# Three head pairs' queries and keys kept in SBUF, a reordered first chunk of products, and one scaling moved from ScalarE to VectorE, in a hybrid attention and pooling block

## The chip, the cores and the metric

The kernel runs on one core of a Trainium2 chip. A core has five engines that run their own instruction streams side by side: TensorE (PE, matrix products; the load of its weights is listed apart as PEld), VectorE (DVE), ScalarE (ACT), GpSimd (POOL) and SyncE (SP, which here only issues transfers). Transfers run on 16 DMA engines. SBUF is the on-chip memory of 128 partitions, PSUM holds the results of the products, DRAM is outside. The metric is the time of one execution in device microseconds, lower is better.

## The reference

One block over 1024 tokens of width 1024, all in float32. The input is normed and projected; the projection's columns feed latent attention of 8 heads (64 plain and 32 rotary dimensions, causal by chunks of 64 tokens), a pooling branch over trailing windows, and gates. Both branches are gated, projected, merged, projected once more, added to the input and normed.

```python
def mla_attention(zq, zkv, zkr, q_norm, w_uq, kv_norm, w_ukv):
    c_q = rms_norm(zq, q_norm)
    q = jnp.einsum('bsr,rhd->bshd', c_q, w_uq)
    q_nope = q[..., :QK_NOPE_DIM]                      # 64 dims
    q_rope = apply_rope(q[..., QK_NOPE_DIM:], ...)     # 32 dims
    kv = jnp.einsum('bsr,rhd->bshd', rms_norm(zkv, kv_norm), w_ukv)
    k_nope, v = kv[..., :QK_NOPE_DIM], kv[..., QK_NOPE_DIM:]
    k_rope = apply_rope(zkr, ...)
    # per block of 128 queries: softmax(mask((qn.kn + qr.kr) * scale)) @ v

def reference(...):
    z = jnp.einsum('bsd,de->bse', rms_norm(x, norm_in), w_in)
    zq, zkv, zkr, g_attn, u_pool, g_pool, g_merge = jnp.split(z, IN_SPLITS, axis=-1)
    y_attn = mla_attention(...) * silu(g_attn)
    y_pool = multiscale_pool(u_pool, ...) * silu(g_pool)
    merged = gate_a * (y_attn @ w_branch_attn) + gate_p * (y_pool @ w_branch_pool)
    return rms_norm(x + merged @ w_out, norm_final)
```

## The kernel before, in words

Every float32 product is made of three products of rounded halves: an operand is split into a rounded part (names `wh`, `hi`, `uh`, `kh`, `qh`, made on ACT at L298) and the rest (`wl`, `lo`, `ul`, `kl`, `ql`, made on DVE at L308), and h·h, h·l and l·h are summed in PSUM (`mms`, L275).

The program's stages in order of time: the first products, `zq`, over eight chunks of the input (0 to some 45 us); the input projection and the pooling branch (to some 360 us); the queries and keys of the four head pairs and the values (`run_up`, `run_rope`, `run_v`, to 394 us); attention head by head (from 394 us to some 555 us), into whose gaps the pooling branch's products `pf` (weights `w_bp`, one piece for each head) are laid; the attention branch's projection, the output projection and the final norm.

The order on each engine comes from `Plan.order` (L127 to L202). It simulates the program with a cost for each operation and takes, on each engine, among the operations that could start within 30 ns of the first the one that stands first in the program. SBUF tiles come from tags with a fixed number of slots (L25): `t`, 45 tiles of 128x1024, `wr` and others. Slots of a tag are handed out in the order in which the program first names the tiles; so a late tile holds up those behind it. `wr` has one slot: the next weight piece can be loaded only when VectorE has made the `wl` of the piece before it. `wh` and `wl` have two each.

All loads and stores of `dma` (L372 to L383, the rows say L378) are issued by SP in this one order, so an issue that waits holds up all behind it. An SP issue also waits until the transfer eight places before it has landed.

The **first chunk**, n = 0 (L610 to L630): x comes in two halves of 512 tokens. ACT makes the rounded half (`xa` left, `xb` right), DVE the rest into the same tiles, and PE multiplies with the rounded weights `wqh` and the rest `wql`. There are 18 products of 128x512: three parts (wh·h, wh·l, wl·h), two halves, three column groups (`ps`, `ps`, `pb`).

**Queries and keys** (`run_up`, L822 to L850): for each pair p of heads the product lies in PSUM, is split into `uh` and `ul` of 128x1024 (64 partitions for each head), and these are written to DRAM (`qn_d`, `kn_d`). Head 0's half goes to the heads' operand tiles straight from `uh` and `ul`. There are two sets of operand tiles (`heads[0]`, `heads[1]`: `qh`, `ql`, `kh`, `kl`); `load_head` (L811) fills the set of head h, 64 partitions from `qn_d` and `kn_d` and 32 from the rotary part. The loads of a head stand in the order behind the last score product of the head that used the set before.

**Attention's start**: each head has score products `sc`, their maxima on DVE (L357), exponentials `pr` on ACT (L290), a scaling on POOL (L322), transposes `pt` on PE (L282), the transposed tile's split `pT` (ACT L298, DVE L308), and the products `o` with the values.

**The end** (`finish`, L1288): two row blocks `res` are left; the one before the last is scaled by one over its norm and written out, while the last still gets its final piece (`pb`, added on DVE) and its squares (`junk`, on ACT).

Of the kernel before, what the change touches and what calls it, by code (L numbers as in the profile page):

```python
# [10 lines left out]
AF = mybir.ActivationFunctionType  # L11
ALU = mybir.AluOpType
AX = mybir.AxisListType

P = 128
# [4 lines left out]
QK_DIM = 96  # L20
Q_RANK = 384
KV_RANK = 256
N_BG = 4
WARM = 8
SLOTS = {"t": 45, "wr": 1, "wh": 2, "wl": 2, "go": 2, "oa": 2, "s": 2, "p": 2, "o": 1, "f": 1}  # L25
PSUM = "spof"
# [183 lines left out]
def hybrid_block_kernel(  # L210
# [42 lines left out]
    def dram(rows, name, cols=T):  # L253
        b = Buf(lambda: tc.dram_tile([rows, cols], F32, name=name), None)
        return View(b, 0, rows, 0, cols)
# [217 lines left out]
    mask_d = dram(64, "mask_d")  # L473
    kr_d = [dram(32, f"kr_d{i}") for i in range(2)]
    qr_d = [[dram(P, f"qr_d{t}{i}") for i in range(2)] for t in range(2)]
    qn_d = [[dram(P, f"qn_d{p}{i}") for i in range(2)] for p in range(4)]
    kn_d = [[dram(P, f"kn_d{p}{i}") for i in range(2)] for p in range(4)]
    gate_d = [dram(P, f"gate_d{t}") for t in range(16)]
    y_d = [dram(P, f"y_d{t}") for t in range(4)]
    gp_d = [dram(P, f"gp_d{t}") for t in range(4)]  # L480
# [78 lines left out]
    zq_acc = [Acc("s"), Acc("s"), Acc("pp")]  # L559
# [44 lines left out]
    for n, k in enumerate(ORDER):  # L604
        w, x = raws[k]
        wh, wl = buf("wh", 1024, F32R, "wqh"), buf("wl", 1024, F32R, "wql")
        xa, xb = tr("xa"), tr("xb")
        if k < 4:
            xs[k] = ((xa[:, :512], xb[:, :512]), (xa[:, 512:], xb[:, 512:]))
            step_n = 512  # L610
        else:
            xs[k] = ((xa[:, :512], xa[:, 512:]), (xb[:, :512], xb[:, 512:]))
            step_n = T
        for a in range(0, T, step_n):
            c = slice(a, a + step_n)
            h, l = (xs[k][0][a // 512], xs[k][1][a // 512]) if k < 4 else (xa, xb)
            act(h, x[:, c], AF.Copy, scale=gin[k])
            if a == 0:
                if n == 0:
                    vcopy(wh[:, :Q_RANK], w[:, :Q_RANK])  # L620
                    tt(wl[:, :Q_RANK], w[:, :Q_RANK], wh[:, :Q_RANK].f32(), ALU.subtract)
                else:
                    split(wh[:, :Q_RANK], wl[:, :Q_RANK], w[:, :Q_RANK])
            stt(l, x[:, c], gin[k], h.f32(), ALU.mult, ALU.subtract)
        if n + 3 < 8:
            raws[ORDER[n + 3]] = start_loads(ORDER[n + 3])
        h, l = xs[k]
        for a, b, f, e in ((wh, h, n == 0, False), (wh, l, False, False), (wl, h, False, n == 7)):
            for hf in range(2):
                mms([(zq_acc[c].halves[hf], a[:, 128 * c : 128 * c + 128], b[hf], f, e) for c in range(3)])  # L630
    for n in range(4):
        B.setdefault("b11", []).append((xs[n][0][0], xs[n][1][0]))
        B.setdefault("b21", []).append((xs[4 + n][0][0], xs[4 + n][1][0]))
# [177 lines left out]
    def load_head(h):  # L811
        d = heads[h % 2]
        p, r = h // 2, 64 * (h % 2)
        load_rope(h)
        for x, n in enumerate("hl"):
            dma(d["q" + n][0:64, :].f32(), qn_d[p][x][r : r + 64, :])
            dma(d["k" + n][0:64, :].f32(), kn_d[p][x][r : r + 64, :])

    def run_up(p, which, first):
        def run(it):  # L820
            acc = next_acc()
            cs = state["cq"] if which == "q" else state["ckv"]  # L822
            n = len(cs)
            if first:
                shared[which] = (it.h, it.l)
            if which == "q" and p == 0:
                for g in range(4):
                    yp[g] = t32("y")
                    dma(yp[g], y_d[g])
                load_mp(0)  # L830
            if which == "k" and p == 1:
                dress_slots(heads[0])
                load_rope(0)
                load_mp(1)
            wh, wl = shared[which]
            o = n * (p if which == "k" else p % 2)
            prod(acc, wh[o : o + n], wl[o : o + n], halves(cs))
            h, l = tr("uh"), tr("ul")
            for ps, a, b in acc.spans:
                split(h[:, a:b], l[:, a:b], ps)  # L840
            dst = qn_d if which == "q" else kn_d
            if p == 0:
                if which == "q":
                    make_slots()
                dma(heads[0][which + "h"][0:64, :].f32(), h[0:64, :].f32())
                dma(heads[0][which + "l"][0:64, :].f32(), l[0:64, :].f32())
            r = 64 if p == 0 else 0
            dma(dst[p][0][r:P, :], h[r:P, :].f32())
            dma(dst[p][1][r:P, :], l[r:P, :].f32())
        return run  # L850

    def run_rope(t):
# [274 lines left out]
    q, kv = Latents("q"), Latents("kv")  # L1127
# [129 lines left out]
    class Rows:  # L1257
# [31 lines left out]
        def finish(self, e, last=False):  # L1289
            r, ss, st = self.t[e], self.ss[e], self.st[e]  # L1290
# [7 lines left out]
            if last and not e:  # L1298
                act(r[:, rgt], r[:, rgt], AF.Copy, scale=st)
                stt(r[:, 256:512], r[:, 256:512], st, nf[:, 256:512], ALU.mult, ALU.mult)  # L1300
                ts(r[:, :256], r[:, :256], st, None, ALU.mult)
            elif last:
                act(r, r, AF.Copy, scale=st)
            else:
                stt(r, r, st, nf, ALU.mult, ALU.mult)
            for c in (lft, rgt):
# [145 lines left out]
    for h in range(HEADS):  # L1452
# [7 lines left out]
        for qr in range(4):  # L1460
            prs = []
            for i in (2 * qr, 2 * qr + 1):
                nk = 128 * (i + 1)
                ps = buf("s", T, F32, "sc")
                q = slice(128 * i, 128 * i + 128)
# [135 lines left out]
```

## Time and profile before

| what | value |
|---|---|
| runs (us) | 701.85, 703.6, 706.39; median 703.6 |
| the profiled execution's own time | 702.37 us |
| its span | 700.2 us, 9698 instructions, mean granted clock 0.991 |
| PE busy | 682.6 us (97%) |
| DVE, ACT, POOL busy | 539.6 (77%), 355.9 (51%), 116.8 us (17%) |
| written to DRAM / read from DRAM | 46.27 MB / 93.73 MB |

Times inside the trace count from the span's start. A row of a timeline gives the start, how long one instruction took (x8: eight together), engine, line, operation, the tile written and the tiles read, and in brackets the idle time of the engine before it and the work that it waited for. The rows that the prediction uses stand in the section behind the change.

### The profile page before, as it was taken

To read this page: it belongs to the slowest core of one execution; us is meant where nothing else is said; L and a number is where in the kernel's file an instruction comes from. 1 tells how busy PE (TensorE), PEld (TensorE's weight loads), DVE (VectorE), ACT (ScalarE), POOL (GpSimd) and SP (SyncE) were. 2 spreads that over 40 slices of the span, in tenths; PEclk is the share of its full clock that TensorE was granted. 3 is DMA by queue.
4 is the path that set the end of the run, shared out by engine and by line. 5 is a ranking of instruction groups with operands and counts; after the bars stand their busy time and mean duration, and the time that the engine had idled before them with its cause. 6 is when DMAs were issued, how large, how long until landed. Compare 5 with 4: busy or idle time off the path is not lost.

```text
span 700.2 us, 9698 instructions
## 1 busy us (share of the span) xinstructions
PE 682.6 (97%) x3368; PEld 574.3 (82%) x3368; DVE 539.6 (77%) x868; ACT 355.9 (51%) x660; POOL 116.8 (17%) x153
## 2 busy tenths in 40 slices
PE   8999999999999999999999979999999999999995
PEld 6878888888888888888888769999899888878784
DVE  5687997668878578669958757877887889967883
ACT  5864524442444354443545546677676673334433
POOL 0020100300003030300001034444444300000000
PEclk9999999999999999999999989999999999999998
DMA  8947656361977539364778982554540389984612
GB/s 314 383 163 278 208 208 189 82 189 59 316 238 191 176 126 321 85 191 149 293 240 301 331 190 62 147 145 112 122 121 31 106 288 372 303 270 134 203 68 90
DMA packets 55871, 136.42 MB, mean 195 GB/s; under 512 B 5904, under 2 KB 17296, under 8 KB 55696
## 3 DMA queue, kind: packets, MB, share of 16 engines
q1 hardware_dynamic: 53568, 131.63, 56.0%
q0 software_dynamic: 2256, 4.20, 4.2%
q8 instruction: 26, 0.43, 0.3%
q14 instruction: 21, 0.17, 0.1%
HBM read 93.73 MB, written 46.27 MB: 200 GB/s over the span
## 4 chain that ended last, share of the span: by engine, by line
PE 88%; DMA 4%; DVE 3%; issue 2%; ACT 1%; SPq 1%; DVEq 0%; ACTq 0%
PE pb L275 36%; PE ps L275 31%; PE sc L275 6%; PE pf L275 5%; PE o L275 5%; PE pt L282 4%; PE pv L275 2%; DMA kh<-kr_d 1%; DMA wr<-w_bp 1%; SPq L378 1%; DMA x<-xT 1%; DVE mr L308 1%; DMA mr<-m_d 1%; DVE small L357 0%; DVE res L308 0%
## 5 line engine op out<-in xcount | busy, mean ns | idle before, releaser
L275 PE MATMUL pb<-t,wp 128*128 128x512 f32 x504 | 121.3, 389 | 0.0
L275 PEld LDWEIGHTS pb<-t,wp 128*128 128x128 f32 x504 | 94.4, 188 | 19.5
L298 ACT CAST wp<-wr 128x512 fp32r<-128x512 f32 x98 | 59.4, 620 | 94.6 <-PE ps L275 53.3
L308 DVE TENSOR_TENSOR wp<-wr,wp 128x512 fp32r<-128x512 f32 x98 | 71.9, 747 | 36.8 <-ACT wp L298 35.5
L275 PE MATMUL ps<-xa,wp 128*128 128x512 f32 x224 | 73.8, 389 | 0.0
L322 POOL TENSOR_SCALAR pr<-pr,small 128x128 f32<-128x128 f32 (+3 forms) x64 | 48.7, 765 | 77.3 <-DVE small L348 68.9
L290 ACT ACTIVATE pr<-sc,small 128x128 f32<-128x128 f32 (+3 forms) x64 | 47.6, 745 | 19.3 <-DVE small L357 16.4
L308 DVE TENSOR_TENSOR pT<-pt,pT 128x512 fp32r<-128x512 f32 (+1 forms) x80 | 48.8, 633 | 8.9 <-ACT pT L298 8.3
L357 DVE TENSOR_REDUCE small<-sc 128x1 f32<-128x128 f32 (+3 forms) x64 | 47.3, 750 | 9.8 <-PE sc L275 9.2
L298 ACT CAST pT<-pt 128x512 fp32r<-128x512 f32 (+1 forms) x80 | 41.5, 544 | 25.5 <-PE pt L282 24.5
L275 PE MATMUL o<-pT,v 128*128 128x256 f32 (+1 forms) x320 | 48.4, 286 | 2.0 <-ACT pT L298 1.5
L275 PEld LDWEIGHTS ps<-xa,wp 128*128 128x128 f32 x224 | 42.0, 188 | 8.7
L275 PEld LDWEIGHTS o<-pT,v 128*128 128x128 f32 x320 | 44.8, 193 | 4.8 <-ACT pT L298 1.9
L275 PE MATMUL ps<-xb,wp 128*128 128x512 f32 x112 | 43.6, 389 | 0.0
L282 PE MATMUL pt<-ident,pr 128*128 128x128 f32 x288 | 42.6, 276 | 0.3 <-DVE pT L308 0.3
L275 PE MATMUL pb<-wo,wp 128*128 128x512 f32 (+1 forms) x180 | 40.5, 376 | 0.2 <-DVE res L308 0.2
L275 PE MATMUL pb<-xa,wp 128*128 128x512 f32 x168 | 40.7, 389 | 0.0
L275 PE MATMUL ps<-t,wp 128*128 128x512 f32 x168 | 40.7, 390 | 0.0
L275 PE MATMUL sc<-kh,qh 128*128 128x384 f32 (+4 forms) x96 | 36.2, 377 | 2.9 <-ACT pr L290 2.8
L275 PEld LDWEIGHTS pb<-wo,wp 128*128 128x128 f32 x180 | 32.4, 188 | 7.0 <-issue 0.5
L275 PEld LDWEIGHTS pb<-xa,wp 128*128 128x128 f32 x168 | 31.5, 188 | 6.5
L275 PEld LDWEIGHTS ps<-t,wp 128*128 128x128 f32 x168 | 31.5, 188 | 6.5
(207 smaller groups left out, 1446.5 us busy)
## 6 DMA issues: line engine op xcount, KB each, us to landing
wr<-w_z SPq DMA_DIRECT2D x30, 512.0 KB, 5.3
gate_d<-z SPq DMA_DIRECT2D x16, 512.0 KB, 3.5
xt<-xr SPq DMA_DIRECT2D x8, 512.0 KB, 9.8
mp<-gate_d SPq DMA_DIRECT2D x8, 512.0 KB, 6.5
gate<-gate_d SPq DMA_DIRECT2D x8, 512.0 KB, 7.4
wo<-wt_d SPq DMA_DIRECT2D x8, 512.0 KB, 9.2
m_d<-gate SPq DMA_DIRECT2D x16, 256.0 KB, 5.7
mr<-m_d SPq DMA_DIRECT2D x16, 256.0 KB, 4.5
```

Of the source, the lines that this page charges most:

```text
L275: nc.tensor.matmul(real(o), real(a), real(b), start=s, stop=e, **kw)
L282: nc.tensor.transpose(real(o), real(a), real(ident))
L290: nc.scalar.activation(real(o), real(x), func, scale=real(scale), **kw)
L298: lambda: nc.scalar.copy(real(o), real(x)),
L308: plan.add(eng, lambda: e.tensor_tensor(real(o), real(a), real(b), op), c, [a, b], [o], port=port)
L322: e.tensor_scalar(real(o), real(a), real(s1), real(s2), op0, op1)
L357: lambda: nc.vector.tensor_reduce(real(o), real(a), axis=AX.X, op=ALU.max, negate=True),
L378: lambda: nc.sync.dma_start(real(o), real(x)),
```

## The change

Three edits. The first chunk's 18 products are written in the program with all three parts of the left half of the tokens first, then all three of the right half (the planner still chooses the order on the engine, below). The queries and keys of head pairs 0 to 2 are no longer written to DRAM: their `uh` and `ul` (12 tiles of the tag `t`) stay in SBUF, and `load_head` copies 64 partitions of them into the heads' operand tiles; pair 3 is written to DRAM and read back as before. The row block before the last is scaled on VectorE (`ts`) where ScalarE (`act`) did it.

```diff
@@ -20,7 +20,7 @@
 QK_DIM = 96
 Q_RANK = 384
 KV_RANK = 256
-N_BG = 4
+KEPT = 3
 WARM = 8
 SLOTS = {"t": 45, "wr": 1, "wh": 2, "wl": 2, "go": 2, "oa": 2, "s": 2, "p": 2, "o": 1, "f": 1}
 PSUM = "spof"
@@ -473,8 +473,8 @@
     mask_d = dram(64, "mask_d")
     kr_d = [dram(32, f"kr_d{i}") for i in range(2)]
     qr_d = [[dram(P, f"qr_d{t}{i}") for i in range(2)] for t in range(2)]
-    qn_d = [[dram(P, f"qn_d{p}{i}") for i in range(2)] for p in range(4)]
-    kn_d = [[dram(P, f"kn_d{p}{i}") for i in range(2)] for p in range(4)]
+    n_d = {w: [dram(P, f"{w}n_d{i}") for i in range(2)] for w in "qk"}
+    nope = {}
     gate_d = [dram(P, f"gate_d{t}") for t in range(16)]
     y_d = [dram(P, f"y_d{t}") for t in range(4)]
     gp_d = [dram(P, f"gp_d{t}") for t in range(4)]
@@ -625,9 +625,11 @@
         if n + 3 < 8:
             raws[ORDER[n + 3]] = start_loads(ORDER[n + 3])
         h, l = xs[k]
-        for a, b, f, e in ((wh, h, n == 0, False), (wh, l, False, False), (wl, h, False, n == 7)):
-            for hf in range(2):
-                mms([(zq_acc[c].halves[hf], a[:, 128 * c : 128 * c + 128], b[hf], f, e) for c in range(3)])
+        parts = ((wh, h, n == 0, False), (wh, l, False, False), (wl, h, False, n == 7))
+        for (a, b, f, e), hf in (
+            [(p, hf) for hf in range(2) for p in parts] if n == 0 else [(p, hf) for p in parts for hf in range(2)]
+        ):
+            mms([(zq_acc[c].halves[hf], a[:, 128 * c : 128 * c + 128], b[hf], f, e) for c in range(3)])
     for n in range(4):
         B.setdefault("b11", []).append((xs[n][0][0], xs[n][1][0]))
         B.setdefault("b21", []).append((xs[4 + n][0][0], xs[4 + n][1][0]))
@@ -813,8 +815,8 @@
         p, r = h // 2, 64 * (h % 2)
         load_rope(h)
         for x, n in enumerate("hl"):
-            dma(d["q" + n][0:64, :].f32(), qn_d[p][x][r : r + 64, :])
-            dma(d["k" + n][0:64, :].f32(), kn_d[p][x][r : r + 64, :])
+            for w in "qk":
+                dma(d[w + n][0:64, :].f32(), nope[w, p][x][r : r + 64, :])
 
     def run_up(p, which, first):
         def run(it):
@@ -838,15 +840,17 @@
             h, l = tr("uh"), tr("ul")
             for ps, a, b in acc.spans:
                 split(h[:, a:b], l[:, a:b], ps)
-            dst = qn_d if which == "q" else kn_d
             if p == 0:
                 if which == "q":
                     make_slots()
                 dma(heads[0][which + "h"][0:64, :].f32(), h[0:64, :].f32())
                 dma(heads[0][which + "l"][0:64, :].f32(), l[0:64, :].f32())
-            r = 64 if p == 0 else 0
-            dma(dst[p][0][r:P, :], h[r:P, :].f32())
-            dma(dst[p][1][r:P, :], l[r:P, :].f32())
+            if p < KEPT:
+                nope[which, p] = h.f32(), l.f32()
+            else:
+                nope[which, p] = n_d[which]
+                for v, o in zip((h, l), n_d[which]):
+                    dma(o, v.f32())
         return run
 
     def run_rope(t):
@@ -1300,7 +1304,7 @@
                 stt(r[:, 256:512], r[:, 256:512], st, nf[:, 256:512], ALU.mult, ALU.mult)
                 ts(r[:, :256], r[:, :256], st, None, ALU.mult)
             elif last:
-                act(r, r, AF.Copy, scale=st)
+                ts(r, r, st, None, ALU.mult)
             else:
                 stt(r, r, st, nf, ALU.mult, ALU.mult)
             for c in (lft, rgt):
```

SP has 308 issues where it had 320: twelve stores to DRAM are gone, four of 256 KB (pair 0: 64 partitions) and eight of 512 KB, 5 MB in all. The planner also moves instructions.

**PE, the first chunk.** The rows from the second product group on, of the kernel before (`xa` is the left half of the tokens, `xb` the right; `wqh` and `wql` the weights' rounded part and rest).

```order
L275 MATMUL ps_130<-xb_136,wqh_126 128x512
L275 MATMUL ps_132<-xb_136,wqh_126 128x512
L275 MATMUL pb_146<-xb_136,wqh_126 128x512
L275 MATMUL ps_130<-xa_121,wqh_126 128x512
L275 MATMUL ps_132<-xa_121,wqh_126 128x512
L275 MATMUL pb_134<-xa_121,wqh_126 128x512
L275 MATMUL ps_130<-xb_136,wqh_126 128x512
L275 MATMUL ps_132<-xb_136,wqh_126 128x512
L275 MATMUL pb_146<-xb_136,wqh_126 128x512
L275 MATMUL ps_130<-xa_121,wql_128 128x512
L275 MATMUL ps_132<-xa_121,wql_128 128x512
L275 MATMUL pb_134<-xa_121,wql_128 128x512
```

The same twelve rows of PE in the changed kernel:

```order
L275 MATMUL ps_130<-xb_136,wqh_126 128x512
L275 MATMUL ps_132<-xb_136,wqh_126 128x512
L275 MATMUL pb_146<-xb_136,wqh_126 128x512
L275 MATMUL ps_130<-xa_121,wqh_126 128x512
L275 MATMUL ps_132<-xa_121,wqh_126 128x512
L275 MATMUL pb_134<-xa_121,wqh_126 128x512
L275 MATMUL ps_130<-xa_121,wql_128 128x512
L275 MATMUL ps_132<-xa_121,wql_128 128x512
L275 MATMUL pb_134<-xa_121,wql_128 128x512
L275 MATMUL ps_130<-xb_136,wqh_126 128x512
L275 MATMUL ps_132<-xb_136,wqh_126 128x512
L275 MATMUL pb_146<-xb_136,wqh_126 128x512
```

A tile `xa` or `xb` holds the rounded part of its half and, in its second 512 columns, the rest; the rows do not tell these apart. The first three rows of both lists are wh·h of the right half and the next three wh·l of the left; only the second group of right products (wh·l) and the products of `wql` with the left half have changed places. The planner took the first right products when it reckoned them ready, ahead of the left rest, in both programs.

**SP, around the load of the second piece of `w_bp`.** `wr` is the weight piece, `kn_d` and `qn_d` are the stores to DRAM, `kh_3118` and `qh_3289` are heads' operand tiles. SP before, from a load of `mp` on:

```order
L378 DMA mp_3144<-gate_d_2270 128x1024
L378 DMA kn_d_3161<-uh_3146 128x1024
L378 DMA kn_d_3164<-ul_3148 128x1024
L378 DMA kn_d_3166<-uh_3150 128x1024
L378 DMA kn_d_3177<-ul_3153 128x1024
L378 DMA wr_3193<-w_bp 128x512
L378 DMA kn_d_3197<-uh_3179 128x1024
L378 DMA kn_d_3210<-ul_3191 128x1024
L378 DMA qh_3289<-mask_d 32x1024
L378 DMA kh_3291<-mask_d 32x1024
L378 DMA kh_3291<-kr_d_517 32x1024
L378 DMA kl_3295<-kr_d_2662 32x1024
```

SP in the changed kernel, from the same load of `mp` on:

```order
L378 DMA mp_3119<-gate_d_2270 128x1024
L378 DMA kl_3106<-ul_3102 64x1024
L378 DMA wr_3169<-w_bp 128x512
L378 DMA kn_d_3173<-uh_3155 128x1024
L378 DMA kn_d_3186<-ul_3167 128x1024
L378 DMA qh_3267<-mask_d 32x1024
L378 DMA qh_3267<-qr_d_3005 32x1024
L378 DMA qh_3267<-uh_2915 64x1024
L378 DMA kh_3271<-mask_d 32x1024
L378 DMA kh_3271<-kr_d_517 32x1024
L378 DMA kh_3271<-uh_3091 64x1024
L378 DMA ql_3275<-qr_d_3019 32x1024
```

The second piece `wr_3169` stands ahead of the two stores that are left of that stretch, where `wr_3193` stood behind four of six; the loads of head 1 (`qh_3267`, `kh_3271`) read `uh` in SBUF.

The third piece stands behind the loads of head 1 in both programs (`wr_3359` before; in the changed kernel `wr_3313`, 14 rows behind the second piece, with the load `ga` ahead of it and a fourth piece right behind it).

**ACT, the start of attention.** ACT before, from the last split of the pooling input (`hi`) on:

```order
L298 CAST hi_3273<-y_2850 128x1024
L298 CAST v_3287<-pv_3260 128x8x64
L290 ACT_TABLE_LOAD
L290 ACTIVATE pr_3323,small<-sc_3275,small 128x128
L290 ACTIVATE pr_3325,small<-sc_3279,small 128x256
L298 CAST wh_3334<-wr_3193 128x512
L298 CAST pT_3357<-pt_3348 128x384
L290 ACTIVATE pr_3364,small<-sc_3327,small 128x384
L290 ACTIVATE pr_3370,small<-sc_3336,small 128x512
```

ACT in the changed kernel, from the same row on:

```order
L298 CAST hi_3249<-y_2850 128x1024
L298 CAST wh_3260<-wr_3169 128x512
L298 CAST v_3265<-pv_3236 128x8x64
L290 ACT_TABLE_LOAD
L290 ACTIVATE pr_3301,small<-sc_3251,small 128x128
L290 ACTIVATE pr_3305,small<-sc_3255,small 128x256
L298 CAST pT_3335<-pt_3328 128x384
L290 ACTIVATE pr_3340,small<-sc_3307,small 128x384
L290 ACTIVATE pr_3346,small<-sc_3316,small 128x512
L298 CAST wh_3355<-wr_3313 128x512
```

The cast `wh<-wr` of the second piece moves from behind the exponentials `pr` of head 0's first two blocks to ahead of the last cast of the values `v`, and the cast of the third piece moves up behind the 128x512 exponentials. On DVE the matching `wl<-wr` moves to behind the first two TENSOR_REDUCE.

On DVE, at the end, the TENSOR_SCALAR of 128x1024 stands between the reciprocal and the last addition from PSUM (`res<-pb,res` 128x256).

## Rows read from the trace of the kernel before

**Rows 1.** Stretches: from:to, its length, busy us of each engine, PEclk granted, DMA share, GB/s.

```profile
10.00:394.00 384.00, 383.97 (x1721) 316.53 (x1720) 298.75 (x419) 186.57 (x292) 46.12 (x36) 1.00 0.65 214
384.00:400.00 16.00, 15.71 (x74) 12.96 (x73) 13.67 (x22) 10.88 (x19) 0.85 (x2) 1.00 0.97 328
402.00:422.00 20.00, 16.07 (x80) 13.92 (x79) 11.35 (x22) 9.57 (x21) 5.79 (x7) 0.83 0.83 192
440.00:540.00 100.00, 98.85 (x670) 90.39 (x669) 80.15 (x169) 69.62 (x163) 47.40 (x64) 1.00 0.43 113
```

**Rows 2.** Timeline, the first chunk.

```profile
7.07 0.72 ACT L290 ACTIVATE xb<-x,vec 128x512 fp32r<-128x512 f32 x1 [1.68 <-DMA x<-xT]
7.83 0.75 DVE L329 SCALAR_TENSOR_TENSOR xb<-x,vec,xb 128x512 fp32r<-128x512 f32 x1 [1.10 <-ACT xb L290]
...
7.85 0.73 PE L275 MATMUL ps<-xb,wqh 128*128 128x512 f32 x2 [1.29 <-ACT xb L290]
...
9.34 0.62 PE L275 MATMUL ps<-xb,wqh 128*128 128x512 f32 x2
...
11.38 0.62 PE L275 MATMUL ps<-xa,wqh 128*128 128x512 f32 x2
```

**Rows 3.** Timeline of PE and ACT, the start of attention.

```profile
402.13 0.39 PE L275 MATMUL pf<-hi,wl 128*128 128x512 f32 x1
...
402.99 0.62 ACT L298 CAST wh<-wr 128x512 fp32r<-128x512 f32 x1 [4.93 <-DMA wr<-w_bp]
...
405.56 0.57 PE L275 MATMUL sc<-kh,qh 128*128 128x320 f32 x1
...
408.88 0.42 PE L275 MATMUL sc<-kh,qh 128*128 128x384 f32 x1
```

**Rows 4.** Timeline of PE and ACT, the start of head 1.

```profile
415.22 0.62 ACT L298 CAST wh<-wr 128x512 fp32r<-128x512 f32 x1 [3.55 <-DMA wr<-w_bp]
...
417.40 0.33 PE L275 MATMUL sc<-kh,qh 128*128 128x128 f32 x1 [1.97 <-ACT pr L290]
...
422.08 0.40 PE L275 MATMUL pf<-hi,wh 128*128 128x512 f32 x1
```

**Rows 5.** Timeline of SP: the issues of the second and third w_bp piece.

```profile
392.93 1.07 SPq L378 DMA_DIRECT2D wr<-w_bp  x1
...
407.52 0.53 SPq L378 DMA_DIRECT2D wr<-w_bp  x1
```

**Rows 6.** Timeline of DVE: wl of the first piece, and head 0's first maxima.

```profile
383.63 0.69 DVE L308 TENSOR_TENSOR wl<-wr,wh 128x512 fp32r<-128x512 f32 x1 [1.28 <-ACT wh L298]
...
396.80 0.61 DVE L357 TENSOR_REDUCE small<-sc 128x1 f32<-128x128 f32 x2
```

**Rows 7.** Transfers of 460 to 500 us: queue, count, KB each, median us from issue to landing.

```profile
mp<-gate_d SPq DMA_DIRECT2D x3, 512.0 KB, 6.5
wr<-w_bp SPq DMA_DIRECT2D x2, 256.0 KB, 2.9
```

**Rows 8.** Transfers of 366 to 425 us.

```profile
kh<-uh SPq DMA_DIRECT2D x1, 256.0 KB, 5.5
```

**Rows 9.** Timeline of PE and DVE, head 1.

```profile
443.31 1.04 PE L275 MATMUL o<-pT,v 128*128 128x256 f32 x8
...
449.57 0.68 DVE L308 TENSOR_TENSOR mp<-pf,mp 128x512 f32<-128x512 f32 x1
```

**Rows 10.** Timeline, the end.

```profile
693.16 0.41 DVE L308 TENSOR_TENSOR res<-pb,res 128x256 f32<-128x256 f32 x1
693.28 1.15 ACT L290 ACTIVATE res<-res,small 128x1024 f32<-128x1024 f32 x1 [0.23 <-DVE small L348]
694.34 0.40 ACT L290 ACTIVATE junk<-res 128x256 f32<-128x256 f32 x1
...
695.99 0.35 DVE L320 TENSOR_SCALAR res<-res,small 128x256 f32<-128x256 f32 x1
```

**Rows 11.** Groups by line and shape: busy us, mean ns of one.

```profile
L320 DVE TENSOR_SCALAR xa<-xa,vec 128x512 f32<-128x512 f32 x4 | 1.9, 482 | 0.0
```

## The prediction

> **What bounds the kernel now.** I read the stretches first, then the timeline inside those that stand out, then the transfers. From 10 to 394 us PE is busy for 383.97 of 384.00 us at a granted clock of 1.00, and in 440 to 540 us for 98.85 of 100.00 [rows 1]. In both, only less work on PE could shorten the time, and the change takes no product away. What is left to win lies before 10 us, in 394 to 422 us (in 402 to 422 PE is busy 16.07 of 20.00 us, granted clock 0.83 [rows 1]), and behind the last product.
>
> At the start PE stands 1.29 us before 7.85 and waits for ACT's `xb`, which itself waited for the right half of x to land [rows 2].
>
> At the start of attention two stalls stand. PE could go on at 402.13 + 0.23 = 402.36 us, and its next score product starts at 405.56; ACT's cast `wh<-wr` had waited 4.93 us, until 402.99, for the second `w_bp` piece [rows 3]. The cast `pT` that PE needs is queued behind it. The second stall is the same with the third piece: ACT waits 3.55 us until 415.22, and with an exponential queued behind that cast PE stands 1.97 us, until 417.40 [rows 4]. The pieces are issued at 392.93 and 407.52 [rows 5] and so take about 10.0 and 7.6 us, where the same load takes 2.9 us in a quieter stretch [rows 7]. The DMA engines are at 0.97 in 384 to 400 us [rows 1]: stores of queries and keys fill them, and on SP, at 1.07 us for an issue [rows 5], four stores of keys stand ahead of the second piece.
>
> **The change, part A (first chunk).** The program asks for the left half first, but the order on PE shows that the first three right products (wh·h) still stand fourth to sixth, ahead of the left rest. PE takes its queue in order, so the wait for `xb` that ends at 7.85 stays whole. What moved is the second right group (wh·l), now three products later. Before, it stood at 9.34, when DVE's rest of `xb` had been ready since 7.83 + 0.75 = 8.58 [rows 2]: nothing waited there. Same 15 products of 0.235 us from 7.85 to 11.38 [rows 2], same first product of the next chunk. **A = 0.** Bounds: 0 both ways, since the only wait is ahead of the rows that moved. Had all nine left products stood first, the 1.29 us would be filled; that is what this part could bring at most.
>
> **Part B (queries and keys kept).** First what the two stalls cost.
> - Gap one: 405.56 - 402.36 = 3.20 us, less four products `o` of half a 512-column product or less (0.47): 2.73.
> - Behind it, at half clock: from 405.56 to 408.88 [rows 3], 3.32 us, stand six score products of 320 columns, three of 384 and seven transposes of 128, 3968 columns; at 0.235 us for 512 columns they take 1.82: 1.50 lost.
> - Gap two: 1.97 [rows 4].
> - Behind it, from 417.40 to 422.08 [rows 4], 4.68 us, stand 3 x 128, 6 x 512, 3 x 128 and 8 x 256 columns, 5888, which take 2.70: 1.98 lost.
>
> That is 8.2. Narrow products cost more than their columns, so I count 7.8 as the most that can come back.
>
> What of it goes? Twelve stores leave SP, most of them between 375 and 394 us. The second piece now stands ahead of the two stores that stay. Its slot is free when DVE has made `wl` of the first piece, at 383.63 + 0.69 = 384.3 [rows 6]. Even with the 10.0 us of before it has landed at 394.3, and ACT reaches its cast, now ahead of the last cast of `v`, after the last product of the values, which ends at 394 us [rows 1]: gap one loses its cause. The cast's 0.62 us [rows 3] delay `v` on ACT, whose partner on DVE was taken behind other work anyway. The matching `wl`, 0.69 us, comes on DVE behind the first maxima, which end at 396.80 + 0.61 = 397.4 [rows 6], and moves the first reciprocal by 0.5; twelve `pf` products (2.8 us) and six scores stand on PE between the first scores and the first transposes and hide that.
>
> The third piece waits for that `wl` (one slot), so it is issued at about 397.4 + 0.69 + 0.1 = 398.2. At the quiet 2.9 us [rows 7] it lands at 401.1, and ACT comes to it behind the 128x512 exponential; without the cast of 402.99 that exponential ends near 402.5. With 7.6 us it would be there at 405.8, 3.3 too late. I take the quiet price, since the loads of head 1, ahead of it on SP, are issued by about 392 and no store stands between.
>
> What does not go: five later heads leave 1.15 us idle in 100 [rows 1], 0.2 each, and both casts now fall into the stretch in which PE has least work in stock. I leave 0.8 for it: **B = 7.0**. Bounds: 7.8, and 3.9 where the third piece's stall (1.97 + 1.98) stays.
>
> Heads 1 to 5 now load from SBUF instead of DRAM. One such copy stands in the rows, `kh<-uh` of 256 KB, 5.5 us in the fullest stretch [rows 8]. A head's four copies, 0.53 us apart [rows 5], are there after 3 x 0.53 + 5.5 = 7.1 us; a head lasts 100 / 5 = 20 us [rows 1], and they are issued one head ahead. Cost nothing: 12 us of slack hide it.
>
> **Part C (the scaling).** ACT takes 1.15 us from 693.28, then come the last squares at 694.34 [rows 10]. No row shows DVE scaling 1024 columns. Rows of the operation: 0.35 us for 256 [rows 10], 0.48 for 512 [rows 11], so 0.5 ns a column and 0.74 for 1024; from below 0.48, from above twice that. It starts like ACT's at 693.28 and ends at 694.02; the last addition from PSUM (0.41 [rows 10]), which ran beside ACT's scaling, now stands behind it and ends at 694.43, and the squares wait for it. **C = -0.1**, between +0.2 (0.48 us) and -0.3 (0.96). [...]
>
> **Sum.** 0 + 7.0 - 0.1 = 6.9 us. From the profiled execution's 702.4 that gives 695.5, from the runs' median 703.6 it gives 696.7; the profiled one lies among the runs, so I take the middle, **696.1 us**.
>
> **Rivals.**
> - *The third piece stays late.* It hangs on DVE's `wl`, one slot and SP's order, with 1.4 us to spare. Against it: nothing large is in flight then. B falls by 1.97 + 1.98, the gain to 2.9: 699.5 to 700.7, by 703.0 (the middle of the two bases) 700.1.
> - *A kept tile holds up a load.* 12 of the 45 slots of `t` stay taken, so others come free later: by the order the slot of the third `mp` load now frees only when the `o` products at 443.31 are done, at 444.2. With 6.5 us [rows 7] it lands at 450.7, where DVE wants it at 449.57 [rows 9], with both ends moved alike by B. Late by 1.1, or by 3.1 with a slow stretch behind it of the size above: 697.2 to 699.2.
> - *The other side: the copies inside SBUF are slow.* Heads 2 to 5 have 20 us each for a set of four. With a set of length L PE stands 4 x (L - 20) us: this outweighs 6.9 from L = 21.7 on and is 1% slower from L = 23.5. At L = 25 the time is 696.1 + 20 = 716. The row's 5.5 us speaks against it. [...]
> - *The stores were not the cause*, the DMA engines stay as full, and nothing changes: 703.0. Against it: 5 MB at the 328 GB/s of 384 to 400 us [rows 1] are 15 us of all DMA engines' time.
>
> **How the numbers follow.** Forecast 0.62, third piece late 0.14, held-up load 0.12, stores not the cause 0.08, slow copies 0.04. The forecast's own range runs from 702.4 - 7.8 - 0.2 = 694.4 to 703.6 - 6.0 = 697.6 (B one lower). The range that leaves out no more than 2 in 10 takes in the held-up load and most of the late piece, and the runs' spread of 0.7 below the median: 693.7 to 700.3. One per cent, about what a measurement of this kernel tells from no change, is 7.0 us: faster means under 696.6, which is some four fifths of the forecast's weight below its upper part, 0.49. Within 1%: the rest of the forecast and the first, second and fourth rival, 0.46. Slower: 0.05.
>
> **What would show it.** A: the wait of about 1.3 us before `ps<-xb,wqh` is still there. B: `wr<-w_bp` is issued near 384 and 398 and lands ahead of its casts, PE is busy over 19 of 20 us in 402 to 422 and its granted clock there is 1.00; the attention stage ends about 7 us earlier. C: the last squares follow DVE's addition. I am wrong if the wait for `xb` is gone, if ACT still waits for `wr<-w_bp`, if PE waits on `mp` or a head's tiles, or if a product group moves for no wait shown here.

## The result, and the profile after

The changed kernel takes **693.48 us** (median of four runs, 692.74 to 694.56) where the kernel before takes 703.55 (701.85 to 706.39): 0.9854 of it, 95% interval 0.9818 to 0.9890, 10.1 us less. I had forecast 696.1, with 693.7 as the lower end. The profiled executions lie closer together than the medians: 702.37 and 694.56 us, 7.8 apart, spans 700.2 and 692.7. (The traces hold 336 issues on SP beside 348; the section on the change has 308 and 320, with the same twelve between them.)

The stretches of the changed kernel (from:to, length, busy us of PE, PEld, DVE, ACT and POOL, PEclk granted, DMA share, GB/s) beside [rows 1]:

```profile
384.00:400.00 16.00, 15.71 (x75) 13.01 (x74) 13.67 (x22) 10.96 (x19) 2.75 (x4) 1.00 1.02 285
402.00:422.00 20.00, 20.00 (x133) 18.44 (x132) 14.43 (x31) 12.50 (x31) 8.81 (x13) 1.00 0.42 107
440.00:540.00 100.00, 98.86 (x669) 90.66 (x668) 80.43 (x169) 68.63 (x161) 46.08 (x62) 1.00 0.35 93
```

PE is busy for all 20.00 us of 402 to 422, where it was for 16.07, and the granted clock there is 1.00 for 0.83. Before, behind the two gaps, where the prediction speaks of half clock, it was 0.61 over the 3.32 us and 0.64 over the 4.68 us, and 0.50 for a part of each (405.90 to 407.00 and 418.67 to 420.00 us); here PE has no such gap. The DMA engines are emptier there (0.42 for 0.83); in 384 to 400 us, where the prediction called them full, they are as full as before (1.02 for 0.97). The five later heads are as before (98.86). What PE waits for in the whole program (us in total, times, longest):

```profile
PE sc L275 <- ACT pr L290: 0.8, 1, 0.8
PE ps L275 <- DVE wp L308: 0.6, 1, 0.6
...
PE pf L275 <- DVE v L308: 0.3, 1, 0.3
```

No wait is over 0.8 us, apart from the start. The loads of the second and third `w_bp` piece on SP (the row of two issues holds the third and, when the slot is free again, the fourth), beside [rows 5]:

```profile
383.69 0.33 SPq L378 DMA_DIRECT2D wr<-w_bp  x1
...
397.41 6.18 SPq L378 DMA_DIRECT2D wr<-w_bp  x2
```

and their casts on ACT, beside the casts of [rows 3, 4]:

```profile
393.68 0.62 ACT L298 CAST wh<-wr 128x512 fp32r<-128x512 f32 x1
...
401.71 0.62 ACT L298 CAST wh<-wr 128x512 fp32r<-128x512 f32 x1
```

Neither cast has waited. The second piece is issued 9.2 us earlier than before, the third 10.1 us. The third was in time by less than 0.1 us: it landed 4.2 us after its issue, near 401.6.

```profile
wr<-w_bp SPq DMA_DIRECT2D x1, 256.0 KB, 4.2
```

(All of the rows at 380 to 402 us are 0.66 us earlier than in the first trace of before for a reason that lies at the start, below.)

The end, beside [rows 10]: the scaling is now VectorE's, the last addition from PSUM behind it, and the last squares behind that.

```profile
685.86 0.75 DVE L320 TENSOR_SCALAR res<-res,small 128x1024 f32<-128x1024 f32 x1
686.53 0.42 DVE L308 TENSOR_TENSOR res<-pb,res 128x256 f32<-128x256 f32 x1
...
687.04 0.42 ACT L290 ACTIVATE junk<-res 128x256 f32<-128x256 f32 x1 [1.41 <-DVE res L308]
```

### The profile page after: what moved, and what is told of

Same layout as the page of the kernel before. It is cut to its first block, busy times and chain, and to the rows that moved or that the text cites. A ratio compares the mean times of both kernels' runs of the same rounds, so it can differ in the third digit from the quotient of the medians.

```text
span 692.7 us, 9705 instructions
## 1 busy us (share of the span) xinstructions
PE 680.2 (98%) x3368; PEld 572.3 (83%) x3368; DVE 540.1 (78%) x869; ACT 355.3 (51%) x659; POOL 116.5 (17%) x153
## 4 chain that ended last, share of the span: by engine, by line
PE 81%; DMA 8%; DVE 6%; issue 2%; ACT 2%; SPq 0%; DVEq 0%; ACTq 0%
PE pb L275 32%; PE ps L275 28%; PE sc L275 7%; PE pf L275 5%; PE o L275 5%; PE pt L282 4%; DMA m_d<-gate 2%; DMA gate<-gate_d 2%; DVE wo L308 1%; DMA ma<-m_d 1%; DMA kn_d<-uh 1%; DVE gate L308 1%; DVE mr L308 1%; DMA mr<-m_d 1%; DMA wq<-w_q 0%
## 5 line engine op out<-in xcount | busy, mean ns | idle before, releaser
L275 PE MATMUL o<-pT,v 128*128 128x256 f32 (+1 forms) x320 | 47.0, 281 | 0.0
## 6 DMA issues: line engine op xcount, KB each, us to landing
xt<-xr SPq DMA_DIRECT2D x8, 512.0 KB, 10.1
```

Source lines behind the costliest of these rows:

```text
L275: nc.tensor.matmul(real(o), real(a), real(b), start=s, stop=e, **kw)
```

## Experiments

**The two kernels again, and what a trace can be compared by.** The runs of one kernel spread: 20 runs of before on one chip lie between 700.83 and 706.27. Traces are finer. From the first score product of head 0 to that of head 2, PE does the same products in every version (a few change places); how long that takes is read from PE's timeline and is called the stretch. It is where part B acts. The expectations of e9, e10 and e12 count it from a row of PE some 7.6 us later (34.8 us for the first trace, where the table has 42.45), so 7.6 us are to be added to their bounds. These are the starts of the two products, and the medians of the runs:

| kernel | head 0, head 2 (us) | stretch | median of the runs | before beside it |
|---|---|---|---|---|
| before, first trace | 394.07, 436.52 | 42.45 | 703.55 | |
| before again (e1) | 392.85, 436.45 | 43.60 | 702.57 (one run) | 703.01 |
| before, third (e12) | 392.87, 437.19 | 44.32 | 702.88 (one run) | 703.5 |
| part A alone (e7) | 395.94, 439.35 | 43.41 | 701.70 | 702.72 |
| stores kept (e3) | 393.40, 435.94 | 42.54 | 701.03 | 703.01 |
| queries kept only (e10) | 398.38, 437.08 | 38.70 | 696.66 | 703.5 |
| keys kept only (e9) | 393.11, 431.51 | 38.40 | 698.28 | 703.5 |
| w_bp by GpSimd's queue (e4) | 395.32, 431.53 | 36.21 | 698.82 | 703.01 |
| changed kernel | 393.40, 428.14 | 34.74 | 693.48 | 703.55 |
| changed kernel again (e5) | 392.61, 427.34 | 34.73 | 693.73 | 702.72 |
| part B alone (e2) | 395.43, 430.15 | 34.72 | 695.28 | 703.01 |
| part B alone again (e6) | 392.94, 427.66 | 34.72 | 692.93 | 702.72 |
| left really first (e8) | 393.00, 427.73 | 34.73 | 692.99 | 702.72 |
| left first, scaling on ACT (e11) | 393.36, 428.10 | 34.74 | 693.07 | 703.5 |

*Before, again and a third time (e1, e12); the changed kernel again (e5).* No edit.

> The kernel before once more, for a second trace. Theory 1 (the two late w_bp pieces cost about 7.7 us in every execution): ACT's cast of the second piece waits for it until about 403 and that of the third until about 415, PE from the last pf at 402 to head 2 in the same places within 1 us. Theory 2 (the wait for the pieces and for the right half of x varies with the transfers' luck, which would explain that the runs' medians lie 10.1 us apart and the two traces only 7.8): the wait for xb or one of the two stalls differs by more than 1 us from the trace shown.

> The kernel before a third time, for its trace: the stretch from the first score product to head 2 took 34.8 us in the first trace, 36.0 in the second, and 35.8 with the first chunk's order alone. If the first trace was the low end, it takes 35 to 36.5 here; if the spread is wider, below 34.8 or above 36.5.

> The changed kernel once more. Theory 1 (the gain is part B, in the same places in every execution; the medians differ by more than the two traces because the kernel before has the larger and more varied stalls): 693 to 695.5 us on this chip, and from the first score product to head 2 PE is again without a wait over 1 us. Theory 2 (the changed kernel's four first runs were lucky at the start): a median of 695 us or more, as the kernel with part B alone had.

The stretch of the kernel before takes 42.45, 43.60, 44.32 us and, with part A alone, 43.41: the first trace, on which the prediction's sum stands, is the shortest of four. Its time is 702.37 all the same, since its first chunk was later than that of e1 and e12. With all three pairs kept the stretch is 34.72 to 34.74 in six traces; e5 gives 693.73 us, as its first theory had it. For e1 the second theory held, that the stalls vary by more than 1 us; e12, at 44.32, lies above the 42.6 to 44.1 that its expectation gave for a first trace at the low end.

The stalls differ in kind too. In e1 gap one is gone and gap two is 6.5 us. PE and ACT in e1:

```profile
401.57 0.36 PE L275 MATMUL sc<-kh,qh 128*128 128x320 f32 x1
```

```profile
414.55 0.62 ACT L298 CAST wh<-wr 128x512 fp32r<-128x512 f32 x1 [8.04 <-DMA wr<-w_bp]
```

The first row is the score product that ends gap one in [rows 3]. It follows head 0's first product by 8.72 us here, 9.10 in e12 and 8.73 in e7, as in the changed kernel (8.75), and by 11.49 only in the first trace. So in three of four traces the third piece costs, nearly alone, more than both pieces cost in the first. How gap two ends in e12, by ACT and PE:

```profile
414.91 0.62 ACT L298 CAST wh<-wr 128x512 fp32r<-128x512 f32 x1 [8.00 <-DMA wr<-w_bp]
...
415.95 1.01 ACT L290 ACTIVATE pr<-sc,small 128x896 f32<-128x896 f32 x1
```

```profile
417.10 0.47 PE L275 MATMUL sc<-kh,qh 128*128 128x128 f32 x1 [6.33 <-DMA ql<-qn_d]
```

PE's row names a load as what came last. That load was issued at 411.56 and is head 2's, and the product is head 1's; what it was held by is the exponential of 415.95 (with its read-out it ends at 417.06), as in [rows 4], and behind that the third `w_bp` piece, for which ACT had waited 8.00 us. In all four traces with this traffic the second gap ends so, with the cast of the third piece and the exponential behind it on ACT.

**Part B alone (e2, e6).** The edit is the change without its first and last part:

```diff
-N_BG = 4
+KEPT = 3
...
+            if p < KEPT:
+                nope[which, p] = h.f32(), l.f32()
...
```

> Part B alone (three head pairs kept), first chunk and last scaling as before. Theory 1: all of the gain, 693 to 695 us, ratio to before 0.985 to 0.990. Rival (the first chunk's order brings something that the trace shows at its start, 0.66 us): 0.7 us slower than the changed kernel, not to be told apart by the time but by the wait of PE before the first ps<-xb,wqh: theory 1 has that depend on when the right half of x lands, in this kernel as in any other.

> Part B alone again, beside the changed kernel on the same chip. If parts A and C are worth nothing, the two medians agree within 0.7 us; if the first chunk's order is worth what separates the first runs of both (695.28 and 693.48), this one is 1.5 to 2 us slower again.

Ratio 0.9904 (0.9888 to 0.9920) in e2 and 0.9859 (0.9838 to 0.9881) in e6. The first is just outside its expectation. The second stands 0.8 us under the changed kernel beside it (692.93 against 693.73; 0.7 was expected at most), so the runs show no gain of parts A and C, and the 1.8 us between the first runs of e2 and of the changed kernel were not an effect of the first chunk's order. The same program gave 695.28 on one occasion and 692.93 on another; in the trace of e2 head 0 starts at 395.43, in that of e6 at 392.94. From there to head 2 the two run alike (34.72); behind head 2 e6 is 0.9 us shorter.

That last part varies between traces of nearly the same program: from head 2 to the end of the span 262.8 us in e6 and 262.9 in e8, 264.6 in the changed kernel's first trace and in e11. The place is at about 620 us, at the start of the output projection: ACT waits for a load `mr`, and PE for the tile `wp` that ACT and DVE make from it. ACT and PE of the changed kernel:

```profile
617.47 0.63 ACT L290 ACTIVATE wp<-mr 128x512 fp32r<-128x512 f32 x1 [0.73 <-DMA mr<-m_d]
```

```profile
621.66 1.20 PE L275 MATMUL ps<-wo,wp 128*128 128x512 f32 x4 [0.61 <-DVE wp L308]
```

ACT's row starts 189.3 us behind head 2's first product here, 189.6 in e11, 187.8 in e6 and 187.7 in e8. PE waits 1.1 us for `wp` in all in e11, 0.25 in e6 and not at all in e8.

**Stores or loads (e3).** The changed kernel, but pairs 0 to 2 are also written to DRAM, as before:

```diff
+    spare = {(w, p): [dram(P, f"{w}s_d{p}{i}") for i in range(2)] for w in "qk" for p in range(KEPT)}
...
             if p < KEPT:
                 nope[which, p] = h.f32(), l.f32()
+                r = 64 if p == 0 else 0
+                for v, o in zip((h, l), spare[which, p]):
+                    dma(o[r:P, :], v[r:P, :].f32())
```

Nothing reads `spare`. The heads read SBUF.

> The changed kernel, but pairs 0 to 2 are also written to DRAM as before (nothing reads these copies); heads 1 to 5 read SBUF. Theory 1 (the stores hold up SP and the DMA engines and so the w_bp pieces): the second piece is issued near 393 and lands near 403 again, and most of the gain is gone, 700 to 703 us. Rival (the loads of the heads from SBUF are what helps): 694 to 696 us.

Ratio 0.9977 (0.9961 to 0.9994): 2 of 10 us are left, and the stretch is 42.54. So it is the stores, and that heads read SBUF instead of DRAM is worth little. The second piece is issued at 391.62 and cast at 400.72, somewhat ahead of the expected places. The stall has taken another form: ACT waits 3.36 us for the second piece but not for the third, and PE's longest wait is for POOL. The rows of POOL and PE:

```profile
401.71 0.95 POOL L370 MEMSET ql<- 32x1024 f32 x1 [52.01 <-DMA kn_d<-uh]
```

```profile
404.07 1.14 PE L282 MATMUL pt<-ident,pr 128*128 128x128 f32 x3 [4.60 <-POOL pr L322]
```

POOL's MEMSET of head 1's operand tile stands in its queue until a store of pair 3's keys has landed, whose tile it takes over, and the scaling `pr` behind it is late. That store is there in the changed kernel too, issued at 384.12 and landed at 390.1; here it stands behind the others, issued at 392.74. So a store can cost in this kernel by its place on SP and by the tile that it holds.

**Place in the queue or fullness (e4).** The kernel before, in which GpSimd issues the second and third piece; all twelve stores stay:

```diff
-            dma(o, self.src)
+            (dma_pool if getattr(self, "by_pool", False) else dma)(o, self.src)
...
+        items[-1].by_pool = t in (1, 2)
```

`dma_pool`, not shown, is `dma` with the issue on GpSimd.

> The kernel before with one thing changed: the second and third w_bp piece are issued by GpSimd's queue and not by SP; all stores stay. If the place behind the stores on SP is what makes the pieces late: the second piece is issued near 384.5 and lands before 394, the third near 404 and lands by 408, gap one goes, gap two mostly: 695 to 698 us. If the fullness of the DMA engines is what makes them late: the second lands near 394 to 398, the third no earlier than 412, and the time is 699 to 703 us.

Ratio 0.9941 (0.9915 to 0.9968), the stretch is 36.21: 7.2 of the 8.7 us are back with not one byte less. The issues on POOL and the cast of the third piece:

```profile
385.88 0.58 POOL L389 DMA_DIRECT2D wr<-w_bp  x1 [34.27 <-DVE wl L308]
...
402.33 0.61 POOL L389 DMA_DIRECT2D wr<-w_bp  x1 [1.48 <-DMA kn_d<-ul]
```

```profile
409.68 0.62 ACT L298 CAST wh<-wr 128x512 fp32r<-128x512 f32 x1 [0.68 <-DMA wr<-w_bp]
```

The DMA engines were as full (0.94 of 402 to 422 us), and the second piece was there in time all the same: what delays it is its place on SP. The third took 7.3 us to land and was late by 0.68; PE waited 1.3 us for head 1's `kl`, which is behind the stores on SP as before. ACT's casts stand in the same places of its order as in the kernel before, the second behind the 128x256 exponential and the third behind the 128x768 one: that the planner moved them in the changed kernel is not needed for the gain.

Counted from head 0's first product, the third piece lands at 14.3 us here and at 21.4 in the mean of the four traces without part B (before, e1, e12, e7). Of these 7.1 us, 1.5 are that its slot is free earlier, 3.5 that it is issued 0.3 us behind that and not 3.8, and 2.0 that it takes 7.3 us and not 9.3. The first two come of the place in the queue (the slot is free when the second piece is done with). For the last, it now goes ahead of head 1's four loads and not behind them; that this is the reason was not tested. Two loads on another queue gained 7.2 us of the stretch, though their own issue takes only 0.58 and 0.61 us: the second piece goes out at 385.88, and at 392.93 in the first trace of before, behind others' issues. The median of the runs, 698.82, lies between the two ranges of the expectation. The runs spread from 695.28 to 703.02, more than the changed kernel's; the traced one (697.08) also lost 2.7 us at 60 to 70 us, behind a wait that only e10's trace has besides. Why the median gains 4.2 us where the stretch gains 7.2 is not shown.

**Which stores (e9, e10).** Only the keys, or only the queries, of pairs 0 to 2 stay on chip:

```diff
-            if p < KEPT:
+            if p < KEPT and which == "k":
```

(and `"q"` in the other; what is not kept goes through DRAM as in the kernel before.)

> The changed kernel, but only the keys of pairs 0 to 2 are kept; their queries go through DRAM as before. SP then has the second w_bp piece ahead of the two key stores that stay, as in the changed kernel. Theory 1 (the key stores ahead of that piece on SP are what makes it late): the stretch from the first score product to head 2 takes 27 to 28.5 us where before took 34.8 to 36.0, and the time is 693 to 696 us. Rival (all store traffic of 375 to 394 us matters, six of the twelve stores are left): half of the gain, 30 to 32 us there and 697 to 699 us.

> The other half: only the queries of pairs 0 to 2 are kept, the keys are written out; the second w_bp piece stands behind four key stores as before. Theory 1: the stretch from the first score product to head 2 takes 33 to 36 us and the time is 700 to 703 us. Rival (traffic): 30 to 32 us there, 697 to 699 us.

My theory was that the four key stores ahead of the second piece are what counts. It fell, and the rival had the size: 38.40 us with the keys kept, 38.70 with the queries kept, each somewhat more than half of the way from 43.4 to 34.7 (the rival's 30 to 32 us are 37.6 to 39.6 in the table's count), ratios 0.9921 (0.9895 to 0.9947) and 0.9917 (0.9890 to 0.9944). ACT with the keys kept, and then with the queries kept:

```profile
405.04 0.62 ACT L298 CAST wh<-wr 128x512 fp32r<-128x512 f32 x1 [3.73 <-DMA wr<-w_bp]
```

```profile
400.91 0.62 ACT L298 CAST wh<-wr 128x512 fp32r<-128x512 f32 x1 [2.16 <-DMA wr<-w_bp]
```

With the keys kept the second piece is in time, and the third, issued at 397.1 as in the changed kernel, takes 7.9 us and is waited for (head 1's loads went out only at 394.1 to 395.9, just ahead of it; in the changed kernel they began at 387.5). With the queries kept it is the other way round: the second is late by 2.16 us, and the third is not waited for. So each half of the stores holds up something else; that head 1's loads are what slows the third piece in e9 is argued from the order of the issues, not shown. Each stretch is that of one trace, and e10's is of the slowest of its eight runs (702.24, median 696.66).

**The first chunk (e7, e8).** Part A alone; and the changed kernel with a dependency for the planner, so that right products stand behind the left rest:

```diff
-            mms([(zq_acc[c].halves[hf], ...) for c in range(3)])
+            mms([(zq_acc[c].halves[hf], ...) for c in range(3)], after=(xs[k][1][0],) if n == 0 and hf else ())
```

> The first chunk's new order alone in the kernel before. Prediction: A = 0, ratio 1.000 within 0.003, and the wait before the first ps<-xb,wqh as long as the right half of x makes it. Rival: A gives 1.3 to 2 us, ratio 0.997.

> The changed kernel with one extra dependency in the planner, so that all nine left products of the first chunk really stand ahead of the nine right ones on PE. By the prediction's part A: where the right half of x lands at 7.0 us the wait for xb is filled and the second chunk starts up to 1.2 us earlier than with the order of the changed kernel; where it lands below 6 us there is nothing to fill and PE instead waits for DVE's rest of the left half: 0 to 0.5 us lost. Median 0 to 1 us under the changed kernel's.

Part A alone gives 0.9988 (0.9968 to 1.0007), which does not shut out the rival's 0.997; the trace decides. In it the right half of x came late, and the wait stands whole (ACT, then PE):

```profile
7.33 0.72 ACT L290 ACTIVATE xb<-x,vec 128x512 fp32r<-128x512 f32 x1 [2.12 <-DMA x<-xT]
```

```profile
8.11 0.73 PE L275 MATMUL ps<-xb,wqh 128*128 128x512 f32 x2 [1.72 <-ACT xb L290]
```

With the left really first (e8) the right half came at 6.00, and there was nothing to fill. In the trace of e11, which has the same order, it came at 7.13:

```profile
7.13 0.72 ACT L290 ACTIVATE xb<-x,vec 128x512 fp32r<-128x512 f32 x1 [1.95 <-DMA x<-xT]
```

```profile
8.62 0.62 PE L275 MATMUL ps<-xb,wqh 128*128 128x512 f32 x2
```

PE has no wait before that row, since nine left products fill the time, and head 0 starts at 393.36. In e2 the right half came at 7.02, the first products took as long, and PE waited:

```profile
7.79 1.22 PE L275 MATMUL ps<-xb,wqh 128*128 128x512 f32 x2 [0.59 <-ACT xb L290]
```

The products go on at 0.43 us behind that wait, up to about 11 us (in e11 up to about 7.5), and head 0 starts at 395.43. So by these two traces the order that the edit was written for gives some 2 us in an execution in which x comes late, more than the wait itself; e8's trace shows no gain where x comes early. The medians (692.99 beside 693.73) don't tell it.

**The scaling back on ScalarE (e11).**

```diff
-                ts(r, r, st, None, ALU.mult)
+                act(r, r, AF.Copy, scale=st)
```

> The changed kernel with the first chunk's left products really first and the scaling at the end back on ScalarE (part C undone). From the last PE rows to the end of the span 8.65 us where the changed kernel has 8.8 (C = -0.14); the time 692.5 to 694 us, not to be told from the changed kernel's by the runs. If part C were worth something on the whole, it is slower than 694.

From the start of the sixth product from the last on PE to the end of the span: 8.69 us here, 8.67 in e2 and e6, which also scale on ACT, against 8.83, 8.82 and 8.83 with the scaling on DVE (the changed kernel, e5, e8). Part C costs 0.15 us; the medians don't show it.

## Why the prediction was right or wrong

*Part A = 0: right.* e6 beside e5, and e7, show no gain, and the wait for `xb` is where it was when x is late. That PE keeps to the order of its rows the first trace of before shows: DVE's left rest was ready at 5.99 + 0.74 = 6.73 us, and PE stood until 7.85 for the right products ahead of it. What the edit could have brought was put too low, at the wait's 1.29 us: the slow products behind such a wait cost as well (e11 beside e2, 2.1 us). The 0.66 us by which the changed kernel's trace was ahead at the start came from x:

```profile
5.75 0.72 ACT L290 ACTIVATE xb<-x,vec 128x512 fp32r<-128x512 f32 x1 [0.41 <-DMA x<-xT]
```

```profile
5.57 1.19 PE L275 MATMUL ps<-xa,wqh 128*128 128x512 f32 x2 [0.34 <-DVE wqh L352]
...
6.99 0.92 PE L275 MATMUL ps<-xb,wqh 128*128 128x512 f32 x2
```

ACT has the right half at 5.75 instead of 7.07 [rows 2], and PE's first products are slow (two in 1.19 us, where the same two took 0.70 in the first trace of before), which costs part of that again. The same program shows both arrivals, in e1 and in the first trace of before.

*Part B = 7.0: this is the step that failed. The mechanism was right, the size was not.* The waits went, and the issues came at 383.7 and 397.4 where I had put them at 384.3 and 398.2 (less 0.66). The term measured 7.7 us by the trace that the sum was made from and 8.7 by the mean of the four traces (43.45 - 34.73). Two things failed in it.

- I took 0.8 off for stalls that might remain, and none did. The 7.8 that I had called the most is, within 0.1, what that execution lost. Narrow products did cost more than their columns there at 128 columns (0.11 us from one score product to the next at 417.57, where 128 of 512 columns at 0.235 are 0.06), but not at 256 (0.11 at 423.36, by columns 0.12).
- I read what the stalls cost from one execution, and gave the range no room for executions in which they cost more: 43.60, 44.32 and 43.41 us against 42.45. The sum of two gaps described that one execution; in the other three the third piece is nearly all of it. That the profiled time was near the median hid this, because its first chunk was late by about as much as its stalls were short.

One price in it was wrong without harm, which was luck. I had the third piece land 2.9 us after its issue, 1.4 us ahead of its cast; it took 4.2 and was in time by less than 0.1 us. In e11 it came too late,

```profile
402.55 0.62 ACT L298 CAST wh<-wr 128x512 fp32r<-128x512 f32 x1 [1.03 <-DMA wr<-w_bp]
```

and still PE lost nothing (stretch 34.74): the work that PE has in stock there covers a cast that is 1 us late, which I had not worked out.

By the four traces the sum would have been 8.7 - 0.1 = 8.6, and 703.55 - 8.6 = 695.0, inside the range; the measured 693.48 is 1.5 lower still. Taken over all traces, four without part B (before, e1, e12, e7) and six with it, head 0 starts 0.5 us earlier (mean 393.9 and 393.5), the stretch is 8.7 shorter, what comes behind head 2 is as long (263.8 and 263.7), and the time outside the span, which I had left alone, is 0.2 shorter (1.96 to 2.17 us in the four, 1.77 to 1.89 in the six). That makes 9.4, where the runs gave 9.0 (e5), 9.8 (e6) and 10.1. The 0.5 lies in the first 14 us, in the arrival of x and the pace of the first products, and is luck; what is left is within the spread of the runs of before. Why the time outside the span shrinks stays open.

*The cause, "stores fill the DMA engines and SP's queue": right in the queue, less in the engines.* e4 keeps all the traffic and gets 7.2 of the 8.7 us back, and the DMA engines of the changed kernel are as full as before in 384 to 400 us (1.02 for 0.97). What the lower share behind that (0.42 for 0.83 in 402 to 422 us) is worth by itself, no run separates. That four key stores are the ones that matter was wrong (e9, e10).

*Part C = -0.1: right*, -0.15. DVE's scaling of 1024 columns took 0.75 us; the line through the rows of 256 and 512 gave 0.74.

*Loads from SBUF cost nothing: right.* No product of a later head waited for them (the five later heads: 98.86 busy of 100, as before), and e3 shows that they gain little either.

*The held-up `mp` load did not come about, by 0.4 us.* The third load of `mp` waited for its tile, as the order had shown, and its row now is

```profile
436.02 0.32 SPq L378 DMA_DIRECT2D mp<-gate_d  x1
```

It landed 4.8 us later, at 440.8, where I had taken 6.5, and DVE wanted it at 441.26:

```profile
441.26 0.68 DVE L308 TENSOR_TENSOR mp<-pf,mp 128x512 f32<-128x512 f32 x1
```

## What to carry to other kernels

When one queue issues all transfers in order, look for what stands behind a batch of stores, not only at what the stores themselves delay: small loads that a cast waits for, with the engine's other work queued behind the cast, were most of the cost here, and moving two loads to another queue gave 7.2 of the 8.7 us of the stretch that dropping 5 MB of stores gave. Read the size of a stall from several executions before a range is built on it, since a time near the median does not say that each of its parts is. And when code is reordered for a planner that chooses for itself, read the emitted order: the first edit's new order did not reach the products that waited.

## What the runs showed of the hardware that I had not expected

The arrival of the right half of x differs by more than 1 us between executions of the same program (ACT begins with it at 5.86 in e1 and at 7.07 in the first trace of before), and the first products on PE sometimes follow one another at 0.43 us, as in e2 up to about 11 us, where in e5 they follow at 0.23 from 7 us on. The profile's granted clock for 6 to 12 us says 1.00 in e2 all the same. In e7 they follow at 0.43 from 9 to 12 us, behind the wait of 1.72 us. Products of 512 columns also follow at 0.43 in the first trace of before from 418.67 to 420.00 us, behind the wait of 1.97, and there the granted clock says 0.50. What makes the pace in e2 is not shown. Together the arrival of x and this pace move the start of all that follows: the same program has head 0 at 395.43 in e2 and at 392.94 in e6, 2.5 us apart, over a quarter of what the change was worth. Of a stall's size, too, one execution says little: 42.45 to 44.32 us for the same stretch.
